# Half of the row tiles' sums of three modulation sets moved from VectorE to TensorE in a kernel's opening

## The chip, the cores and the metric

The kernel runs on one core of one Trainium2 chip. Its time is the device time of one execution in microseconds (us), and smaller is better. The core has a matrix engine (TensorE, PE in the profile; its weight loads are listed as PEld), a vector engine (VectorE, DVE), a scalar engine (ScalarE, ACT), GpSimd (POOL) and a queue engine (SyncE, SP) that issues most DMA transfers.

## The reference

The model is a trunk of two decoder layers on 512 tokens of width 2048, in float32. The first layer is differential attention, the second forgetting attention over shared keys and values. What the opening of the kernel computes is this:

```
c_act = silu(c)                                    # 2048 values
mod = c_act @ w_mod[0] + b_mod[0]                  # 2048 x 6144 weights
shift, scale, gate = split(mod, 3)
h = x * (1.0 + scale) + shift                      # 512 x 2048
proj = h @ a_w_in                                  # 2048 x 8192 weights; q, k, v, g
```

The product `c_act @ w_mod[0]` reads 2048 x 4096 weights for shift and scale alone, 33.5 MB, and uses each of them once. The projection behind it needs the finished `h`, one block of 128 columns at a time.

## The kernel before

Every large product is made of three float32r products of a high and a low part (`products`, lines 172 to 176), so a 128 x 128 block against 512 columns costs three matmuls. A weight tile comes by DMA as `wst`, ScalarE rounds it into `whi` (line 94) and VectorE subtracts to get `wlo` (line 95).

The opening (lines 438 to 644) has to make `h` before the projection can run, and runs both side by side. The 16 column blocks of shift and scale (`kt` = 0 to 15) are grouped into nine sets (`sets`, line 266): two of one block and seven of two blocks. For each set the opening does the following, in the steps that the code names:

- `load_mods` (line 462) loads the set's weights as tiles `sms` of 1 MB each. A tile of set 0 or 1 holds 8 of the 16 row tiles (128 rows each), so these sets have two `sms` tiles; a tile of the other sets holds 4, so they have four. Five `sms` buffers go round (`NBUF`), and a load waits in SP's queue until its buffer has been read. The block of `x` (`xt`) is loaded along with some of them.
- `mod_steps` (line 484) is a generator. Each step is one VectorE instruction that scales one row tile by its value of `c_act` and adds it to `sacc` (lines 496 and 498). `dv(n)` (line 506) takes up to n of these steps, and stops at the set after the one last summed.
- `mod_sums(i)` (line 512) takes what is left of the set's steps, and then adds `sacc` over its 128 partitions on TensorE, one matmul against a column of ones for each of shift and scale and each column block (line 528). `on_pe(i)` says how many of the 16 row tiles TensorE sums by itself: for these there is no VectorE step, but one matmul of a 128 x 128 weight block against a one-column `cact` (line 525). Before the change this is 8 row tiles for set 1 and none for the other sets.
- `mod_columns` (line 531) adds the bias on VectorE and gives `mcol` (line 534).
- `turn_x(kt)` transposes a block of `x` on TensorE (line 539), and ScalarE writes `hh` and `htmp` from it with scale and shift of `mcol` (lines 543 and 544). `lower_h` makes the low part `hl` on VectorE (line 548).
- `first_products(u, kt, ...)` (line 553) is 21 matmuls against 512 columns for head `u` (0 or 1) and block `kt`. Head 0 takes blocks 0 to 3, then head 1 blocks 0 to 7, and so on (`phases`).

The order of these steps is written out by hand in the string `START` (line 31): a digit is `dv`, `c` is sums, `m` is columns, `t` is turn, `l` is lower, `s` is the split of a weight tile, and `g` is the products of the next block. `turn` takes columns, and sums that are missing, by itself. VectorE's instructions keep exactly the order in which the string traces them; on the other engines a scheduler settles the order within the limits of the data. Each engine works its own instructions strictly in order. After the opening (from line 647 on) nothing depends on the string.

Of the kernel before, what the change touches and what calls it, by code (L numbers as in the profile page):

```python
# [10 lines left out]
F32 = mybir.dt.float32  # L11
# [5 lines left out]
P = 128  # L17
# [10 lines left out]
ET = mybir.EngineType  # L28


START = "cmtlssg6c6t1lgcst4g3tsl9sggts8sl6s2gtggts7lgsstlgg2s7gstl2ss9gsgtslgg5stgg6lsstg2gss8sggt2g4l4sgstctslggtslssggssgggg"
LAM_INIT = 0.8 - 0.6 * math.exp(-0.0)


# [76 lines left out]
def tile_yoco(  # L111
# [44 lines left out]
    def acc_bank(name="acc"):  # L156
        return ps.tile([P, 512], F32, name=name, tag="acc", bufs=4)
# [281 lines left out]
    with tc.tile_pool(name="start", bufs=2, reuse_waits="tile") as sp, tc.manual_schedule(engines={ET.DVE}):  # L439
# [3 lines left out]
        def load_x(q, f0, f1):  # L443
            if f0 == 0:
                xts[q] = sp.tile([P, TB, T], F32, name="xt", tag="xt", bufs=2)
            src = x[:, 512 * q + f0 : 512 * q + f1]
            nc.sync.dma_start(xts[q][:, :, f0:f1], src.rearrange("(b p) f -> p b f", p=P))

        def on_pe(i):
            return 8 if i == 1 else 0  # L450


        tiles = []
# [6 lines left out]
        NBUF = 5  # L460

        def load_mods(upto):
            while state["next"] < min(upto, len(tiles)):
                i, k, nr = tiles[state["next"]]
                k0, nk = sets[i]
                t = sp.tile([P, nr, 2, nk * P], F32, name="sms", tag="sms", bufs=NBUF)
                step = nr // 2 if i < 2 else nr
                for kq in range(0, nr, step):
                    for v in range(2):
                        rows = w_mod[0, (k + kq) * P : (k + kq + step) * P, v * D + k0 * P : v * D + (k0 + nk) * P]  # L470
                        nc.sync.dma_start(t[:, kq : kq + step, v, :], rows.rearrange("(k p) n -> p k n", p=P))
                loaded[i, k] = t
                state["next"] += 1
                if k == 0:
                    if k0 == 0:
                        load_x(0, 0, P)
                    elif k0 == 1:
                        load_x(0, P, T)
                    elif k0 % 4 == 0:
                        load_x(k0 // 4, 0, T)  # L480

        accs = {}

        def mod_steps():
            for n, (i, k, nr) in enumerate(tiles):
                k0, nk = sets[i]
                load_mods(n + NBUF)
                if k >= KT - on_pe(i):
                    continue
                if k == 0:  # L490
                    accs[i] = sp.tile([P, 2, 2 * P], F32, name="sacc", tag="sacc", bufs=2)
                acc = accs[i][:, :, : nk * P]
                for kq in range(nr):
                    w, sc = loaded[i, k][:, kq, :, :], cact[:, k + kq : k + kq + 1]
                    if k + kq == 0:
                        V.tensor_scalar(acc, w, sc, None, op0=ALU.mult)
                    else:
                        V.scalar_tensor_tensor(acc, w, sc, acc, op0=ALU.mult, op1=ALU.add)  # L498
                    yield i

        load_mods(2)
        ws.load(2)
        steps = mod_steps()
        ahead = [next(steps)]

# [6 lines left out]
        def mod_sums(i):  # L512
            k0, nk = sets[i]
            nr = 8 // nk
            dv(-1)
            state["set"] = i + 1
            load_mods(max(n for n, t in enumerate(tiles) if t[0] == i) + 1)
            pm = tr_bank()
            for v in range(2):
                for j in range(nk):  # L520
                    js = slice(j * P, (j + 1) * P)
                    dst = pm[:, nk * v + j : nk * v + j + 1]
                    for k in range(KT - on_pe(i), KT):
                        kr = k // nr * nr
                        PE.matmul(
                            dst, loaded[i, kr][:, k - kr, v, js], cact[:, k : k + 1], start=k == KT - on_pe(i), stop=False
                        )
                    PE.matmul(dst, accs[i][:, v, js], ones[:, 0:1], start=on_pe(i) == 0, stop=True)
            return pm
# [20 lines left out]
        acc = {}  # L550
# [71 lines left out]

        for tok in START:
            if tok.isdigit():
# [391 lines left out]
    npool, n, nstats = zp  # L1016
# [81 lines left out]
    acc = [acc_bank() for _ in range(TB)]  # L1098
# [277 lines left out]
```

## Time and profile before

| | |
|---|---|
| time, median of 3 runs | 1996.07 us (1995.78 to 1996.25) |
| the profiled execution's own time | 1992.9 us |
| its span | 1991.1 us |
| TensorE busy | 1955.8 us, 98% of the span |
| VectorE busy | 1320.8 us, 66% |
| ScalarE busy | 708.2 us, 36% |
| TensorE's granted clock, mean | 0.995 of full speed |

In the views below, the first two numbers of a timeline row are the start and the length in us; then come the engine, the line of the code, the operation, the tile written and those read, and the count. In square brackets stands how long the engine sat idle ahead of the row and what ended that. In a table by stage the columns are the stretch, its length, each engine's busy time with its count of instructions, the clock that TensorE was granted, the share of time in which the DMA engines were busy, and GB/s. Float32 matmuls against one column are recorded as two instructions each.

### The profile page before, as it was taken

The page shows a single profiled execution, that of the slowest core. Times are in us where ns is not written, and L with a number is a line of the kernel's source. Part 1 is how long each engine was busy: PE and PEld are TensorE (multiplying, and loading weights), DVE is VectorE, ACT ScalarE, POOL GpSimd, SP SyncE. Part 2 cuts the span into 40 slices and gives each one's busy share as a digit, 9 for nine tenths or more (in the row PEclk, how much of TensorE's full clock was granted, in tenths as well). Part 3 has the DMA queues.
Part 4 walks back from the last instruction along what each step waited for, and adds up shares of the span by engine and source line. Part 5 has one row for each costly group of instructions (what it writes and reads, how often), then busy time and mean ns, then how long its engine had stood idle before and what let it go on. Part 6 is the DMA issues. An engine that isn't in the chain of part 4 may idle for free.

```text
span 1991.1 us, 24748 instructions
## 1 busy us (share of the span) xinstructions
PE 1955.8 (98%) x9079; PEld 1618.8 (81%) x9079; DVE 1320.8 (66%) x2404; ACT 708.2 (36%) x1217; POOL 2.2 (0%) x10
## 2 busy tenths in 40 slices
PE   5999999999999999999999999999999999999997
PEld 4888888888888888888888888888888888888886
DVE  7885667777777778853575656565555555576657
ACT  2432445333332334431273222224343434353123
POOL 0000000000000000000000000000000000000000
PEclk8999999999999999999999999999999999999999
DMA  9993444666667576552336676663333232232622
GB/s 344 348 317 96 143 149 157 191 213 201 211 191 227 186 232 203 189 170 98 127 128 227 233 239 199 223 212 127 96 96 100 96 105 92 96 120 96 232 92 106
DMA packets 259029, 343.81 MB, mean 173 GB/s; under 512 B 18614, under 2 KB 163404, under 8 KB 258140
## 3 DMA queue, kind: packets, MB, share of 16 engines
q1 hardware_dynamic: 256528, 338.02, 52.0%
q10 hardware_dynamic: 2380, 4.21, 0.6%
q8 instruction: 71, 1.16, 0.2%
q14 instruction: 50, 0.41, 0.1%
HBM read 329.51 MB, written 12.66 MB: 172 GB/s over the span
## 4 chain that ended last, share of the span: by engine, by line
PE 91%; DVE 4%; DMA 2%; issue 1%; ACT 1%; SPq 0%; DVEq 0%; ACTq 0%
PE acc L174 26%; PE acc L176 26%; PE acc L175 26%; PE sc L174 2%; PE sc L175 2%; PE sc L176 2%; PE o L176 1%; PE o L174 1%; PE o L175 1%; PE tr L1228 1%; DMA ms<-in_w_mod_dram 1%; DVE wlo L95 1%; DMA ms<-in_kv_w_mod_dram 1%; DVE sacc L498 1%; DVE macc L391 1%
## 5 line engine op out<-in xcount | busy, mean ns | idle before, releaser
L95 DVE TENSOR_TENSOR wlo<-wst,whi 128x1024 fp32r<-128x1024 f32 (+2 forms) x322 | 384.2, 1195 | 335.5 <-ACT whi L94 319.5
L94 ACT CAST whi<-wst 128x1024 fp32r<-128x1024 f32 (+2 forms) x322 | 331.8, 1031 | 662.2 <-PE acc L176 347.9
L174 PE MATMUL acc<-whi,hh 128*128 128x512 f32 x1232 | 484.3, 396 | 1.8 <-DVE sg L695 1.0
L175 PE MATMUL acc<-wlo,hh 128*128 128x512 f32 x1232 | 480.9, 390 | 0.1
L176 PE MATMUL acc<-whi,hl 128*128 128x512 f32 x1232 | 480.5, 390 | 0.0
L174 PE MATMUL acc<-hh,whi 128*128 128x512 f32 x1184 | 471.1, 398 | 0.6 <-DVE sg L695 0.6
L175 PE MATMUL acc<-hl,whi 128*128 128x512 f32 x1184 | 462.3, 390 | 0.0
L176 PE MATMUL acc<-hh,wlo 128*128 128x512 f32 x1184 | 461.7, 390 | 0.0
L174 PEld LDWEIGHTS acc<-whi,hh 128*128 128x128 f32 x1232 | 232.5, 189 | 48.5 <-DVE ztmp L926 1.2
L176 PEld LDWEIGHTS acc<-whi,hl 128*128 128x128 f32 x1232 | 231.3, 188 | 49.2
L175 PEld LDWEIGHTS acc<-wlo,hh 128*128 128x128 f32 x1232 | 231.6, 188 | 45.4 <-DVE wlo L95 0.5
L176 PEld LDWEIGHTS acc<-hh,wlo 128*128 128x128 f32 x1184 | 222.3, 188 | 48.8
L174 PEld LDWEIGHTS acc<-hh,whi 128*128 128x128 f32 x1184 | 222.6, 188 | 43.8 <-issue 1.9
L175 PEld LDWEIGHTS acc<-hl,whi 128*128 128x128 f32 x1184 | 222.8, 188 | 38.9
L391 DVE SCALAR_TENSOR_TENSOR macc<-ms,cact,macc 128x512 f32<-128x512 f32 x300 | 224.1, 747 | 37.6 <-DMA ms<-in_kv_w_mod_dram 21.8
L498 DVE SCALAR_TENSOR_TENSOR sacc<-sms,cact,sacc 128x512 f32<-128x512 f32 (+1 forms) x127 | 89.5, 704 | 5.0 <-DMA sms<-in_w_mod_dram 1.4
L725 ACT ACTIVATE e<-e,mn 128x128 f32<-128x128 f32 (+3 forms) x64 | 36.1, 564 | 120.6 <-DVE mn L721 120.5
L1217 ACT ACTIVATE eb<-eb,mnb 128x128 f32<-128x128 f32 (+1 forms) x64 | 36.0, 563 | 95.3 <-DVE mnb L1214 94.2
L1214 DVE CUSTOM_DVE_ANT_0 eb<-sc,biasb 128x128 f32<-128x128 f32 (+1 forms) x64 | 31.4, 490 | 55.3 <-PE sc L176 55.3
L1232 DVE TENSOR_TENSOR pTl<-tr,pTh 128x128 fp32r<-128x128 f32 (+1 forms) x64 | 31.1, 487 | 25.3 <-ACT pTh L1231 24.8
L391 DVE SCALAR_TENSOR_TENSOR macc<-msk,cact,macc 128x512 f32<-128x512 f32 x60 | 45.0, 749 | 1.4
L1231 ACT CAST pTh<-tr 128x128 fp32r<-128x128 f32 (+1 forms) x64 | 27.2, 424 | 44.3 <-PE tr L1228 43.5
(260 smaller groups left out, 1773.3 us busy)
## 6 DMA issues: line engine op xcount, KB each, us to landing
wst<-in_a_w_in_dram SPq DMA_DIRECT2D x240, 256.0 KB, 3.8
ms<-in_w_mod_dram SPq DMA_DIRECT2D x64, 512.0 KB, 4.4
ms<-in_kv_w_mod_dram SPq DMA_DIRECT2D x64, 512.0 KB, 4.2
wst<-in_kv_w_dram SPq DMA_DIRECT2D x64, 512.0 KB, 3.9
wst<-in_b_w_in_dram SPq DMA_DIRECT2D x128, 256.0 KB, 2.9
sms<-in_w_mod_dram SPq DMA_DIRECT2D x56, 512.0 KB, 6.9
wst<-in_a_w_out_dram SPq DMA_DIRECT2D x32, 512.0 KB, 3.7
msk<-in_w_mod_dram SPq DMA_DIRECT2D x64, 256.0 KB, 5.5
```

What stands on the lines that cost most here:

```text
L94: self.nc.scalar.copy(hi[:, :, :w], st[:, :, :w])
L95: self.nc.vector.tensor_tensor(lo[:, :, :w], st[:, :, :w], hi[:, :, :w].bitcast(F32), op=ALU.subtract)
L174: PE.matmul(dst, lhs[0], rhs[0], start=start, stop=False)
L175: PE.matmul(dst, lhs[0], rhs[1], start=False, stop=False)
L176: PE.matmul(dst, lhs[1], rhs[0], start=False, stop=stop)
L391: ins = V.scalar_tensor_tensor(acc, w, cact[:, kt : kt + 1], acc, op0=ALU.mult, op1=ALU.add)
L498: V.scalar_tensor_tensor(acc, w, sc, acc, op0=ALU.mult, op1=ALU.add)
L725: S.activation(e[:, :w], e[:, :w], AF.Exp, bias=mn, scale=-1.0, accum_out=rs)
L1214: V.tensor_tensor_reduce(out=e[:, :w], in0=sc[:, :w], in1=bias[:, :w], scale=-1.0, scalar=3.0e38, op0=ALU.add, op1=ALU.min, accum_out=mn)
L1217: S.activation(e[:, :w], e[:, :w], AF.Exp, bias=mn, scale=-1.0, accum_out=rs)
L1231: S.copy(pTh[:, 0 : i + 1, ts], src)
L1232: V.tensor_tensor(pTl[:, 0 : i + 1, ts], src, pTh[:, 0 : i + 1, ts].bitcast(F32), op=ALU.subtract)
```

## The change

`on_pe` returns 8 for the sets 0, 1 and 2 instead of for set 1 alone. For set 0 (one block) and set 2 (two blocks) half of the row tiles, the rows 1024 to 2047, are therefore summed by TensorE at line 525 (527 after the change), and VectorE has 8 steps fewer in each. The generator `mod_steps` now yields ahead of each operation and not behind it, so loads, the allocation of `sacc` and the operation itself are all traced when the step is taken. The head of `START` is written anew; from the characters `sl9sggts8sl6s` on it is as it was.

```diff
-START = "cmtlssg6c6t1lgcst4g3tsl9sggts8sl6s2gtggts7lgsstlgg2s7gstl2ss9gsgtslgg5stgg6lsstg2gss8sggt2g4l4sgstctslggtslssggssgggg"
+START = "cmtlssgc6t2lgcsst3lg3tsl9sggts8sl6s2gtggts7lgsstlgg2s7gstl2ss9gsgtslgg5stgg6lsstg2gss8sggt2g4l4sgstctslggtslssggssgggg"
...
         def on_pe(i):
-            return 8 if i == 1 else 0
+            return 8 if i < 3 else 0
...
         def mod_steps():
             for n, (i, k, nr) in enumerate(tiles):
                 k0, nk = sets[i]
-                load_mods(n + NBUF)
                 if k >= KT - on_pe(i):
                     continue
-                if k == 0:
-                    accs[i] = sp.tile([P, 2, 2 * P], F32, name="sacc", tag="sacc", bufs=2)
-                acc = accs[i][:, :, : nk * P]
                 for kq in range(nr):
+
+                    yield i
+                    if kq == 0:
+                        load_mods(n + NBUF)
+                    if k + kq == 0:
+                        accs[i] = sp.tile([P, 2, 2 * P], F32, name="sacc", tag="sacc", bufs=2)
+                    acc = accs[i][:, :, : nk * P]
                     w, sc = loaded[i, k][:, kq, :, :], cact[:, k + kq : k + kq + 1]
                     if k + kq == 0:
                         V.tensor_scalar(acc, w, sc, None, op0=ALU.mult)
                     else:
                         V.scalar_tensor_tensor(acc, w, sc, acc, op0=ALU.mult, op1=ALU.add)
-                    yield i
```

In the built program this gives TensorE 48 more one-column matmuls (16 in set 0 and 32 in set 2), and VectorE 16 fewer steps. The instruction orders differ as follows. In SP's queue six loads of `wst` stand ahead of the `sms` tiles of row tiles 4 to 11 of set 2; before they stood behind them. On VectorE the bias of set 1 stands behind the second step on the tile of row tiles 4 to 7 of set 2, and all eight VectorE steps of set 2 then end four instructions ahead of that set's bias; the first step of set 3 stands behind the bias of set 2, ahead of which it stood before. On TensorE the transposes for block 3 stand behind the products of block 2, where they stood in the midst of them; and the sums of set 3 stand 78 large matmuls behind those of set 2, where it was 59.

## The prediction

> **What bounds the kernel now.** I read the page's head first, then TensorE's waits in two halves, then the opening's timeline engine by engine, then the granted clock by stage.
>
> ```profile
> span 1991.1 us, 24748 instructions
> PE 1955.8 (98%) x9079; PEld 1618.8 (81%) x9079; DVE 1320.8 (66%) x2404; ACT 708.2 (36%) x1217; POOL 2.2 (0%) x10
> ```
>
> TensorE is the bound: it is busy all but 35 us of the span. A change can only pay if it takes work from TensorE or shortens its few waits. Its waits in the first 43.4 us, and then from there to 220 us, beyond the opening's last set:
>
> ```profile
> PE tr L528 <- DVE sacc L498: 11.1, 1, 11.1
> PE sc L174 <- ACT hh L543: 3.3, 3, 1.6
> ...
> PE tr L539 <- DVE mcol L534: 1.9, 3, 1.0
> PE tr L528 <- ACT whi L94: 1.0, 1, 1.0
> ...
> PE sc L174 <- ACT hh L543: 0.9, 1, 0.9
> ```
>
> The last row is all there is after 43.4 us (it is the wait that ends at 43.34). So from the products of block 2, which start at 43.34, TensorE never stops, and whatever delays that start delays the end by as much, unless later work shrinks. The question is only when these products start after the change, and whether TensorE stays fed behind them.
>
> TensorE's own rows of the stretch:
>
> ```profile
> 14.40 0.99 PE L528 MATMUL tr<-ones,sacc 128*128 128x1 f32 x4 [11.07 <-DVE sacc L498]
> ...
> 14.60 0.78 PE L528 MATMUL tr<-ones,sacc 128*128 128x1 f32 x3
> ...
> 14.82 0.57 PE L528 MATMUL tr<-ones,sacc 128*128 128x1 f32 x2
> ...
> 16.04 1.12 PE L539 MATMUL tr<-ident,xt 128*128 128x128 f32 x4 [0.65 <-DVE mcol L534]
> 18.02 1.22 PE L174 MATMUL sc<-hh,whi 128*128 128x512 f32 x2 [0.87 <-ACT hh L543]
> ...
> 21.17 0.63 PE L175 MATMUL o<-hl,whi 128*128 128x512 f32 x1
> 21.60 1.05 PE L176 MATMUL sc<-hh,wlo 128*128 128x512 f32 x2
> ...
> 23.28 0.39 PE L175 MATMUL acc<-wlo,hh 128*128 128x512 f32 x1
> 23.51 0.39 PE L176 MATMUL acc<-whi,hl 128*128 128x512 f32 x1
> ...
> 25.10 1.84 PE L525 MATMUL tr<-cact,sms 128*128 128x1 f32 x16
> 26.80 0.36 PE L528 MATMUL tr<-ones,sacc 128*128 128x1 f32 x2
> 27.02 1.93 PE L525 MATMUL tr<-cact,sms 128*128 128x1 f32 x16
> 28.81 0.36 PE L528 MATMUL tr<-ones,sacc 128*128 128x1 f32 x2
> 30.18 1.11 PE L539 MATMUL tr<-ident,xt 128*128 128x128 f32 x4 [1.01 <-DVE mcol L534]
> 32.87 1.22 PE L174 MATMUL sc<-hh,whi 128*128 128x512 f32 x2 [1.58 <-ACT hh L543]
> ...
> 39.19 0.39 PE L176 MATMUL acc<-whi,hl 128*128 128x512 f32 x1
> 40.53 1.02 PE L528 MATMUL tr<-ones,sacc 128*128 128x1 f32 x8 [0.96 <-ACT whi L94]
> 41.81 0.66 PE L539 MATMUL tr<-ident,xt 128*128 128x128 f32 x4 [0.26 <-DVE mcol L534]
> 43.34 1.22 PE L174 MATMUL sc<-hh,whi 128*128 128x512 f32 x2 [0.87 <-ACT hh L543]
> ```
>
> The reader sees a chain that repeats: sums, bias, transposes, ScalarE, products. Sixteen one-column instructions and two more against the ones take 1.92 us in set 1 (25.10 to 27.02), 0.107 us each. Those of set 0 start at 14.40, 14.60 and 14.82, some 0.21 us apart: half as fast. The large matmuls do likewise, 0.43 us apart at 21.17 and 0.23 at 23.28. The clock by stage (its column reads 1.00 ahead of 22.7, but these distances say half):
>
> ```profile
> 22.72:26.14 3.42, 3.42 (x22) 1.00 1.09 385
> 26.14:29.55 3.41, 3.03 (x28) 1.00 1.09 386
> 29.55:32.96 3.41, 1.20 (x5) 0.50 1.10 375
> 32.96:36.38 3.42, 3.42 (x8) 0.50 1.09 384
> 36.38:39.79 3.41, 3.19 (x14) 1.00 1.08 397
> 39.79:43.20 3.41, 1.68 (x12) 1.00 1.07 387
> 43.20:46.61 3.41, 3.27 (x8) 0.50 1.09 380
> ```
>
> In these rows the clock changes at the ends of stretches of 3.41 us, and follows the stretch just past. After 32.96 to 36.38, full of large matmuls, it is full. After 26.14 to 29.55 it is halved, though TensorE was busy for 3.03 of 3.41 us, nearly all of it with one-column matmuls. So these rows say that one-column sums don't hold the clock. The DMA engines are saturated all along (1.07 to 1.10, about 385 GB/s).
>
> **Set 0.** VectorE loses 8 steps of 128x256, 4.13 us by this row, in which the second tile had landed by about 10.1 us in its first half:
>
> ```profile
> 10.12 4.13 DVE L498 SCALAR_TENSOR_TENSOR sacc<-sms,cact,sacc 128x256 f32<-128x256 f32 x8 [0.19 <-DMA sms<-in_w_mod_dram]
> ```
>
> TensorE gains 16 matmuls, 32 instructions, which with the four it had run at the halved clock: 36 x 0.213 = 7.7 us. Starting between 9.3 (one DMA earlier) and 10.1, they end at 17.0 to 17.8, against 15.39 before. About 0.35 us comes back, because before the bias stood behind a VectorE step. Block 0's products start about 1.3 us later (19.3); as the clock rises at 22.7 either way, half of that is left when the sums of set 1 start: 25.8 for 25.10. These sums end at about 29.8 (before 29.17).
>
> **Set 1's bias.** Here the delay so far doesn't count, since something later takes over. The bias stands behind two steps on row tiles 4 to 7 of set 2, and their load now stands behind six loads of `wst`. When it lands can be read from a transfer of before:
>
> ```profile
> 31.31 0.83 ACT L94 CAST whi<-wst 128x768 fp32r<-128x768 f32 x1 [12.67 <-DMA wst<-in_a_w_in_dram]
> ...
> 29.97 0.15 DVE L534 TENSOR_TENSOR mcol<-tr,bcol 128x2 f32<-128x2 f32 x1
> ...
> 34.13 6.25 DVE L498 SCALAR_TENSOR_TENSOR sacc<-sms,cact,sacc 128x512 f32<-128x512 f32 x8
> ```
>
> By 31.3 the queue had moved two `sms` tiles (2.10 MB) and one `wst` tile (0.39 MB) behind row tiles 0 to 3 of set 2. After the change the wanted tile is complete after three `wst` tiles (1.31 MB) and itself (1.05 MB), 0.13 MB less: 0.35 us earlier, 30.95. Two steps at 0.78 us (6.25 / 8) give 32.5, and the bias falls at about 32.45 instead of 29.97. Transposes follow 0.21 us later (29.97 to 30.18) and take 1.11, and 0.86 us lies between their end and the products (17.16 to 18.02). Products start at 34.65 instead of 32.87: only 1.8 of the 2.5 us, since before a cast of ScalarE (the row at 31.31) stood in between, which is early now. If the clock rises at 36.4 as before, 4 matmuls run at 0.43 and 17 at 0.2275: end at 40.3. If it rises one stretch later, at 39.8, the end is 41.9.
>
> **Set 2, the main term.** VectorE loses 8 steps, the 6.25 us above, and has its half done by 34.1. All the weights are there by 36.4: two more tiles, 2.10 MB at 385 GB/s, behind the one of 30.95. But TensorE reaches these sums only at 40.3, when before the last VectorE step had just ended too (40.3). It now has 36 matmuls, 72 instructions, in place of 8: nothing covers them, because the next block's transposes wait for the bias behind them. At the full clock they take 72 x 0.109 = 7.9 us, at the half 72 x 0.213 = 15.3. From the row of 26.14 to 29.55 I take a fall at the end of the stretch that starts at 39.8: 27 instructions to 43.2 and 45 x 0.213 = 9.6 us behind it. End at 52.9, against 41.55. Bias, transposes at half clock and ScalarE take 2.2 us (15.39 to 18.02 less the 0.35), so block 2's products start at 55.1 in place of 43.34: **+11.8 us**. Both run their first 3.4 us or so at the half clock; no difference.
>
> **Block 3's transposes** stand behind these products, no longer among them, so the wait for ScalarE is open (0.87 us in the row at 43.34): **+0.9 us**.
>
> **Behind that.** The work that VectorE does between two biases, beside the steps:
>
> ```profile
> 40.70 0.95 DVE L95 TENSOR_TENSOR wlo<-wst,whi 128x768 fp32r<-128x768 f32 x1
> ...
> 45.38 0.68 DVE L548 TENSOR_TENSOR hl<-htmp,hh 128x512 fp32r<-128x512 f32 x1
> 45.99 1.22 DVE L95 TENSOR_TENSOR wlo<-wst,whi 128x1024 fp32r<-128x1024 f32 x1
> ```
>
> Its order puts all of set 3 behind set 2's bias, so its 16 steps start at 53 and not at 40.3, and SP's queue is held: the loads that reuse the buffers of row tiles 8 to 15 of set 2 wait for TensorE's sums to end, all later ones behind them. TensorE has 78 large matmuls between these sums and the next, 17.7 us, so set 3 is covered (16 steps, 12.3 us, and 3.3 for two low parts and two splits). For set 4 the order leaves 61, 13.9 us with 1.7 of transposes and sums, against some 16.2 us of VectorE's work (one split more): short by about half a microsecond, and the low part of one weight tile stands behind eight steps of that set (6.2 us and two splits of 1 us against some 7.3 us of TensorE's work: a wait of 1). Later sets are near balance. The lower end is 0, as the trace of before shows no such wait; the upper end is some 5, five sets with a microsecond each. I take the two shortfalls, 1.5, and 1 more for the DMA queue that stood still: **+2.5 us**.
>
> **The sum.** 11.8 + 0.9 + 2.5 = 15.2 us. The set 0 delay is inside the first term. The arrangement behind the opening is the same, and TensorE is saturated there, so nothing gives it back. The profiled execution took 1992.9 us, of which 1.8 lie around its span; the median of the runs is 3.2 us higher. The difference is added to the median: 1996.07 + 15 = 2011.
>
> **The rivals.** *The sums hold the clock.* The Trainium skill's page "TensorE: Matmul & The Clock Gate", section "What's actually happening", ties the full clock to how busy the engine has been in the last window, without a difference by width. As a mechanism of this kernel: 72 instructions at 0.109 from 40.3 end at 48.15; warm, 1.8 us follow as before (41.55 to 43.34), so products start at 49.9, 6.6 us late, and they save about 1.6 us, as their first 3.4 us don't run at half rate. With 0.9 and 2.5 behind it: +8.4, 2004.5. The fall at 29.55 after a stretch 89% busy speaks against it.
>
> *One-column matmuls are cheaper than the row.* At half its price, 0.054 us, set 2's sums end at 44.2 and the products start at 46.0, warm: 2.7 less 1.6, and 3.4 behind it: +4.5, 2000.6. The 16 in 1.70 us at the full clock (25.10 to 26.80) speak against it: they are the same shape from the same kind of tile. The same page, section "Back-to-back issue gap", gives a floor of about 25 ns for narrow matmuls; by it, as an estimate, the 72 would take 1.8 us and the sum would come to about +2.4.
>
> *Faster.* VectorE was late, and TensorE sums while it would wait. The place is the stretch from 29.2 to 43.3, in which TensorE stood idle for 4.7 us (the five brackets from 30.18 to 43.34). It pays if set 2's sums end before 41.55, so that at 0.109 they begin before 33.7: 6.6 us ahead of what I find, and before the last tile lands. Were it so, the 1.1 us between 39.4 and 40.5 and a microsecond more would be saved: 1994. Decisive is that TensorE reaches these sums at 40.3 with nothing left to wait for.
>
> *No change:* the added sums fit wholly into waits, and VectorE's 10.4 us fewer (4.13 + 6.25) pay for the rest: 1996. It needs an idle TensorE of 10 us between 29 and 43; there are 4.7.
>
> *Worse:* the order behind 53 us falls out of step with the held DMA queue, each set waiting for its loads by 1 to 2 us: +20, 2016 to 2020.
>
> **How the numbers follow.** The likeliest case has 0.62 and spans 2007 to 2016 (15.2 with the later waits 0 or 5, the clock's phase 3 us either way). The warm sums have 0.22 (2002 to 2007), the cheap ones 0.04, faster 0.04, no change 0.03, worse 0.05. The range from 2003 to 2016.5 leaves out faster, none, cheap, worse and a little of the warm case, under 0.2. Repeated runs differ by 0.02%, and about 0.2% (4 us) is what a measurement tells from no change. All cases but faster, none and half of the cheap are slower by more: slower 0.92, same 0.05, faster 0.03.
>
> **What would show it.** Right: some 7 us of one-column matmuls from about 9.5 us; set 1's bias at 32 to 33 behind a wait for `sms`; 72 one-column instructions from about 40 that take 10 to 13 us, with a granted clock of 0.5 from 43 on; block 2's products at 53 to 56; VectorE idle behind the bias of set 2; DMA below 1.0 between 50 and 60; a few waits of TensorE for `sacc` or `wlo` between 70 and 180. Wrong: set 2's sums over by 42, or a full clock through them, or an end less than 5 us later although block 2 starts 10 us late, which would mean that something behind the opening has slack that I don't see.

## The result and the profile after

The changed kernel takes 2010.67 us (median of 6 runs, 2008.68 to 2014.10); the kernel before took 1996.11 in the same series (1995.78 to 1997.05). The ratio is 1.0074, with a 95% interval from 1.0061 to 1.0087: the change makes the kernel slower by 14.6 us. The profiled execution took 2011.02 us.

The head of the page, and then TensorE's waits from 0 to 70 us and from 70 to 230 us:

```profile
span 2009.2 us, 24919 instructions
PE 1974.9 (98%) x9175; PEld 1636.9 (81%) x9175; DVE 1312.4 (65%) x2388; ACT 708.3 (35%) x1217; POOL 2.2 (0%) x10
```
```profile
PE tr L527 <- DVE sacc L501: 6.3, 1, 6.3
PE tr L541 <- DVE mcol L536: 3.7, 3, 3.2
PE sc L174 <- ACT hh L545: 3.5, 4, 0.9
...
PE acc L175 <- DVE wlo L95: 0.8, 1, 0.8
```

TensorE has 96 instructions more and is busy for 19.1 us more, for a span that is 18.1 us longer. On balance, then, the time did not go into waiting. It went into TensorE's own rows in the opening:

```profile
9.69 3.54 PE L527 MATMUL tr<-cact,sms 128*128 128x1 f32 x16 [6.33 <-DVE sacc L501]
13.10 0.56 PE L530 MATMUL tr<-ones,sacc 128*128 128x1 f32 x2
13.52 3.55 PE L527 MATMUL tr<-cact,sms 128*128 128x1 f32 x16
16.93 0.56 PE L530 MATMUL tr<-ones,sacc 128*128 128x1 f32 x2
...
33.90 1.12 PE L541 MATMUL tr<-ident,xt 128*128 128x128 f32 x4 [3.19 <-DVE mcol L536]
35.88 1.22 PE L174 MATMUL sc<-hh,whi 128*128 128x512 f32 x2 [0.87 <-ACT hh L545]
...
43.20 1.84 PE L527 MATMUL tr<-cact,sms 128*128 128x1 f32 x16
44.90 0.36 PE L530 MATMUL tr<-ones,sacc 128*128 128x1 f32 x2
45.12 1.93 PE L527 MATMUL tr<-cact,sms 128*128 128x1 f32 x16
46.91 0.36 PE L530 MATMUL tr<-ones,sacc 128*128 128x1 f32 x2
47.13 2.86 PE L527 MATMUL tr<-cact,sms 128*128 128x1 f32 x16
49.85 0.56 PE L530 MATMUL tr<-ones,sacc 128*128 128x1 f32 x2
50.27 3.55 PE L527 MATMUL tr<-cact,sms 128*128 128x1 f32 x16
53.69 0.56 PE L530 MATMUL tr<-ones,sacc 128*128 128x1 f32 x2
54.51 1.11 PE L541 MATMUL tr<-ident,xt 128*128 128x128 f32 x4 [0.25 <-DVE mcol L536]
56.49 1.22 PE L174 MATMUL sc<-hh,whi 128*128 128x512 f32 x2 [0.87 <-ACT hh L545]
...
65.22 0.73 PE L174 MATMUL sc<-hh,whi 128*128 128x512 f32 x2 [0.87 <-ACT hh L545]
```

The sums of set 2 last from 43.20 to 54.25, 11.05 us, where they took 1.02. No row among them waits for anything. Block 2's products start at 56.49 for 43.34 (13.15 us late), block 3's at 65.22 for 50.18 (15.04 late). The row of before for block 3:

```profile
50.18 0.62 PE L174 MATMUL sc<-hh,whi 128*128 128x512 f32 x2
```

The clock in the stretches of set 2's sums:

```profile
41.07:44.49 3.42, 3.42 (x23) 1.00 1.08 389
44.49:47.90 3.41, 3.41 (x32) 1.00 1.10 380
47.90:51.31 3.41, 3.41 (x18) 0.50 0.53 187
51.31:54.73 3.42, 3.17 (x15) 0.50 0.39 115
```

In the second row TensorE is busy for all of 3.41 us with one-column matmuls, and at its end the clock is halved. In the two rows behind it the DMA engines work at half their share or less, since SP's queue is held until these sums have read their buffers (its longest wait for them is 7.1 us).

### The profile page after: what moved, and what is told of

Same layout as the page of the kernel before. It is cut to its first block, busy times and chain, and to the rows that moved or that the text cites. A ratio compares the mean times of both kernels' runs of the same rounds, so it can differ in the third digit from the quotient of the medians.

```text
span 2009.2 us, 24919 instructions
## 1 busy us (share of the span) xinstructions
PE 1974.9 (98%) x9175; PEld 1636.9 (81%) x9175; DVE 1312.4 (65%) x2388; ACT 708.3 (35%) x1217; POOL 2.2 (0%) x10
## 4 chain that ended last, share of the span: by engine, by line
PE 91%; DVE 4%; DMA 2%; SPq 1%; issue 1%; ACT 1%; DVEq 0%; ACTq 0%
PE acc L174 26%; PE acc L175 26%; PE acc L176 26%; PE sc L174 2%; PE sc L175 2%; PE sc L176 2%; PE o L174 1%; PE o L175 1%; PE o L176 1%; PE tr L1230 1%; DVE wlo L95 1%; DMA ms<-in_kv_w_mod_dram 1%; SPq L471 1%; DMA sms<-in_w_mod_dram 1%; DVE macc L391 1%
## 5 line engine op out<-in xcount | busy, mean ns | idle before, releaser
L391 DVE SCALAR_TENSOR_TENSOR macc<-ms,cact,macc 128x512 f32<-128x512 f32 x300 | 224.4, 748 | 34.2 <-DMA ms<-in_kv_w_mod_dram 18.1
L501 DVE SCALAR_TENSOR_TENSOR sacc<-sms,cact,sacc 128x512 f32<-128x512 f32 (+1 forms) x111 | 79.7, 718 | 6.5 <-DMA sms<-in_w_mod_dram 3.2
```

The source lines that it names most:

```text
L391: ins = V.scalar_tensor_tensor(acc, w, cact[:, kt : kt + 1], acc, op0=ALU.mult, op1=ALU.add)
```

## The experiments

**Which part costs.** Four kernels take the parts one by one. The first has set 2 back on VectorE:

```diff
-            return 8 if i < 3 else 0
+            return 8 if i < 2 else 0
```

> The changed kernel with set 2 back on VectorE (its 32 one-column matmuls gone, 8 VectorE steps back); set 0 and the new order stay. Before is 1996.1 us, the changed kernel 2010.7. Theory A, set 2's sums stand open on TensorE (11.8 of 15.2 us): block 2's products start near 45 us instead of 56.5, and the end is 1999 to 2002. Theory B, the new order itself costs most, whoever sums: the products of block 2 are early again, but the end stays above 2005, with new waits behind 60 us.

The second has only the new string and the new yield:

```diff
-            return 8 if i < 3 else 0
+            return 8 if i == 1 else 0
```

> The changed kernel with sets 0 and 2 both back on VectorE: only the new string and the new place of the yield are left. Theory A: the 3.4 us of the terms for block 3's transposes and for what stands behind, so 1998 to 2001, and block 2's products start at 43 to 45 us. Theory B (the order costs most): 2004 to 2008, with TensorE waiting for sacc or wlo between 60 and 180 us.

The third is the changed kernel with the `START` of the kernel before, and nothing else changed.

> The changed kernel with the old string: TensorE takes half of the sums of sets 0, 1 and 2, the order of steps is the old one. Theory A: 11.8 us of open sums remain, less the terms of the order, so 2007 to 2010, and block 2's products start at 53 to 57 us. Theory B: 1996 to 1999.

The fourth adds set 2's price to the kernel before, as work whose result nothing reads:

```diff
                     PE.matmul(dst, accs[i][:, v, js], ones[:, 0:1], start=on_pe(i) == 0, stop=True)
+                    if i == 2:
+                        spare = pm[:, 64 + nk * v + j : 65 + nk * v + j]
+                        for k in range(8, KT):
+                            PE.matmul(spare, loaded[i, k // nr * nr][:, k % nr, v, js], cact[:, k : k + 1], start=k == 8, stop=k == KT - 1)
```

> The kernel before with the price of set 2 alone: 32 one-column matmuls on the same weights are added to its sums in set 2 and write to a spare column that nothing reads; VectorE, the string and the loads stay as before. Theory A: 64 instructions at 0.107 us as far as the clock lasts and 0.213 behind it, 7 to 13.6 us, all of it open: 2004 to 2009, and the clock falls to half during or right after them. If one-column sums held the clock: +6.8 less up to 1.6, so about 2002, with a clock of 1.00 through them. If they were hidden: 1996 to 1997.

| kernel | median us (runs) | ratio to before, 95% interval |
|---|---|---|
| before, in this series | 1995.16 (18) | |
| set 2 on VectorE | 1999.05 (9) | 1.0022 [1.0012, 1.0032] |
| order alone | 1998.10 (10) | 1.0016 [1.0006, 1.0025] |
| split with the old string | 2008.98 (4) | 1.0070 [1.0055, 1.0085] |
| dead sums in the kernel before | 2007.39 (4) | 1.0061 [1.0046, 1.0076] |

All four times lie where theory A has them (the third inside its 2007 to 2010). Block 2's products start at 46.64 us in the first kernel and at 45.64 in the second, later than theory A had them (near 45, and 43 to 45). The new order alone costs some 3 us; set 2's one-column matmuls, added to a kernel that is otherwise untouched, cost 12. Theory B falls. The clock by stage of the kernel with the dead sums:

```profile
38.18:41.59 3.41, 3.18 (x19) 1.00 1.06 400
41.59:45.01 3.42, 3.42 (x33) 1.00 1.09 385
45.01:48.42 3.41, 3.41 (x18) 0.50 0.53 186
48.42:51.83 3.41, 3.41 (x17) 0.50 0.00 0
```

Again a stretch that is full of one-column matmuls (the second row, with the first sums at 40.81) is followed by half the clock; and the loads stop altogether in the fourth. The order's cost is open rows too. In the profile of the kernel with the order alone, TensorE waits for VectorE's steps of set 2, and block 3's transposes stand behind block 2's products:

```profile
41.67 1.02 PE L530 MATMUL tr<-ones,sacc 128*128 128x1 f32 x8 [2.30 <-DVE sacc L501]
...
45.64 1.22 PE L174 MATMUL sc<-hh,whi 128*128 128x512 f32 x2 [0.87 <-ACT hh L545]
...
52.39 0.60 PE L541 MATMUL tr<-ident,xt 128*128 128x128 f32 x4
53.86 0.73 PE L174 MATMUL sc<-hh,whi 128*128 128x512 f32 x2 [0.87 <-ACT hh L545]
```

Block 2's products thus start 2.3 us later than before, and block 3's 3.7 us. From there to 230 us TensorE waits for nothing. Theory A's 3.4 us for the order was near the measured 2.9, but most of it, the 2.5 us behind the opening's sums, did not arise where theory A had it; that the number fits is luck.

**Is it the width that loses the clock?** The dead sums are replaced by wide matmuls of about the same length at full clock:

```diff
+                    if i == 2:
+                        for k in range(10):
+                            PE.matmul(pm[:, 128:512], Hh[0][:, 0:P], Hh[0][:, 0:384], start=True, stop=True)
```

> The kernel before with 40 dead matmuls of 128x384 in set 2's sums, 6.9 us at full clock, in place of the 32 dead one-column ones, which took 6.8 us by the same clock and brought 2007.4 against 1995.2. Theory A, one-column matmuls don't hold the clock and wide ones do: no fall to 0.5 in or behind these sums, block 2's products start near 50 us and save the 1.6 us of their first stretch: 1999.5 to 2001.5. If the clock fell for another reason (the waits around the sums): 2005 to 2008 again.

It took 2000.68 us (5 runs) against 1994.37, ratio 1.0031 [1.0019, 1.0044]. The stretches around the sums, which run from 42.5 to 50.6:

```profile
42.20:45.60 3.40, 3.31 (x21) 1.00 1.09 383
45.60:49.00 3.40, 3.40 (x23) 1.00 1.09 380
49.00:52.40 3.40, 2.27 (x15) 1.00 1.09 385
```

The clock stays up through them and the products behind. Block 2's products start at 52.39, where near 50 was expected: the sums began 2.0 us later than before (42.53 for 40.53), as set 1's bias had come at 31.80 instead of 29.97, behind waits for `sms`. The lengths at full clock can be read from the first rows of the dead one-column sums and of the wide ones:

```profile
41.02 1.93 PE L532 MATMUL tr<-cact,sms 128*128 128x1 f32 x16
42.81 0.36 PE L528 MATMUL tr<-ones,sacc 128*128 128x1 f32 x2
```
```profile
42.74 1.98 PE L531 MATMUL tr<-hh 128*128 128x384 f32 x10
44.56 0.28 PE L528 MATMUL tr<-ones,sacc 128*128 128x1 f32 x2
```

Sixteen one-column instructions take 1.79 us and ten wide ones 1.82, so 7.2 and 7.3 us in all; yet the first cost 12.2 us and the second 6.3. The wide ones differ in more than the width: they are float32r, one instruction each, and read the same weights every time, where the sums are float32 and read new weights. That the single column alone loses the clock is therefore not shown. This also bears on the Trainium skill's page "TensorE: Matmul & The Clock Gate", section "What's actually happening", where a busy engine is at full clock: if busy means the time in which matmuls run, the rows of this case differ from it (3.41 of 3.41 us busy, and 0.50 behind it).

**Half the size.** Set 2 with a quarter of its row tiles on TensorE:

```diff
-            return 8 if i < 3 else 0
+            return (8, 8, 4)[i] if i < 3 else 0
```

> The changed kernel with a quarter of set 2's row tiles on TensorE in place of half: 16 one-column matmuls instead of 32, 4 VectorE steps back. Without set 2's split the end was 1999.05 us, with half of it 2010.67. If the price went by the count alone, half of the 11.6 us: 2004.9. By theory A it is less than half, since 40 instructions at 0.107 us (4.3 us) fit into the time that the clock still lasts, and a wait for the second half's load is not in the way: block 2's products start near 49 us, and the end is 2001.5 to 2004.

2003.42 us (4 runs), 1.0043 [1.0026, 1.0060]. That is 4.4 us above the kernel without set 2's split, and another 7.2 us come with the second half. The sums take 5.3 us (41.63 to 46.97), and the clock falls only at 45.12, when some 30 of their 40 instructions are through; block 2's products start at 49.21 and run at half clock until 55.36.

**What set 0 costs.** I expected next to nothing from it.

```diff
-            return 8 if i < 3 else 0
+            return 8 if i in (1, 2) else 0
```

> The changed kernel with set 0 back on VectorE; set 2 stays split and the new order stays. Theory A: the delay of set 0 is swallowed by the later bias of set 1, and set 2's sums stay open, so 2008 to 2011, within 2 us of the changed kernel. If set 0's 7.7 us of sums at half clock were on the path: 2004 to 2007.

2005.83 us (4 runs), 1.0057 [1.0042, 1.0072]: 4.8 us less than the changed kernel, so this expectation of theory A was a miss. SP's rows show that more than the sums had changed. Here are the changed kernel, and then the one with set 0 on VectorE:

```profile
14.55 6.34 SPq L471 DMA_DIRECT2D sms<-in_w_mod_dram  x6
20.93 3.33 SPq L47 DMA_DIRECT2D wst<-in_a_w_in_dram  x6
```
```profile
14.42 7.33 SPq L471 DMA_DIRECT2D sms<-in_w_mod_dram  x8
21.79 4.47 SPq L47 DMA_DIRECT2D wst<-in_a_w_in_dram  x6
```

Two loads, the tile with row tiles 4 to 7 of set 2, are ahead of the six `wst` loads again. Loads are now traced with VectorE's first step on a tile. The second tile of set 0 has no step on VectorE any more, and so its call, which loads up to the sixth tile, is gone; a later tile's step makes up for it, too late. To part the two effects, the next kernel keeps set 0 on TensorE and gives the call back (and those of the tiles of sets 1 and 2 that have no VectorE step):

```diff
                 if k >= KT - on_pe(i):
+                    load_mods(n + NBUF)
                     continue
```

> The changed kernel with one line more: for a tile that has no VectorE steps, the loads of the tile five further on are traced where the generator passes it, as in the kernel before, so that the load of set 2's row tiles 4 to 7 stands ahead of the six loads of wst again. The arithmetic stays as in the changed kernel. Taking set 0 off TensorE had saved 4.9 us (2005.83 against 2010.67) and had moved this load too. Theory D, the load is what costs: set 1's bias comes at 30 to 31 us in place of 33.7, and the end is 2004.5 to 2007. If the 7.7 us of sums of set 0 at half clock cost by themselves: the end stays at 2009 to 2011.

2005.50 us (4 runs), 1.0054 [1.0040, 1.0068], with set 1's bias at 30.92. Its rows on VectorE, after those of the changed kernel:

```profile
32.23 1.54 DVE L501 SCALAR_TENSOR_TENSOR sacc<-sms,cact,sacc 128x512 f32<-128x512 f32 x2 [2.48 <-DMA sms<-in_w_mod_dram]
33.69 0.15 DVE L536 TENSOR_TENSOR mcol<-tr,bcol 128x2 f32<-128x2 f32 x1
```
```profile
27.10 3.90 DVE L502 SCALAR_TENSOR_TENSOR sacc<-sms,cact,sacc 128x512 f32<-128x512 f32 x5
30.92 0.16 DVE L537 TENSOR_TENSOR mcol<-tr,bcol 128x2 f32<-128x2 f32 x1
```

And its rows on TensorE:

```profile
53.79 1.22 PE L174 MATMUL sc<-hh,whi 128*128 128x512 f32 x2 [0.87 <-ACT hh L546]
...
58.03 0.60 PE L542 MATMUL tr<-ident,xt 128*128 128x128 f32 x4
...
60.77 0.61 PE L174 MATMUL sc<-hh,whi 128*128 128x512 f32 x2
```

So the late load costs, as theory D has it, and set 0's 7.7 us of sums on TensorE cost nothing that these runs resolve (2005.50 with them, 2005.83 without). How much the load costs is less sure. The time is 5.2 us below the changed kernel's; but above the kernel before, each in its own series, the two stand 14.56 and 11.13 us, a difference of 3.4, and their intervals overlap. In the profiles block 2's products start 2.7 us earlier (53.79 for 56.49), and block 3's 4.5 (60.77 for 65.22). The added line changed TensorE's order too: block 3's transposes stand among block 2's products again (58.03), so the wait of 0.87 us is gone, and the half clock lasts 3.5 us into these products instead of 5.1.

With set 2 on VectorE, set 0 cost only 0.95 us (1999.05 against 1998.10), though its load was late there too. Block 1's products start 2.6 us later (35.46 for 32.85), but block 2's only 1.0 (46.64 for 45.64), since in both kernels TensorE waits for VectorE's steps of set 2, until 43.13 and 41.67. The costs don't add up one by one; what a delay costs depends on which engine is late behind it.

**Why the runs spread.** The changed kernel's runs lie 5.4 us apart.

> The changed kernel once more, for a second profile: its runs spread over 5.4 us, those of the kernel before over 1.3 in the same series. Theory C, the clock's 3.41 us stretches lie differently in each execution, and so do the one-column sums in them: this profile shows its falls and rises shifted by up to 3.4 us against the first, with the same sums at another mean duration, and the span moves with the time spent at half clock. If the spread came from the loads: the same clock, and longer waits for sms.

The two runs took 2009.81 and 2012.40 us, the second with the profile (span 2010.6, 1.4 us longer than in the first profile). Its opening shows the signs of both theories: the clock fell at 47.10 in place of 47.90, and set 2's sums took 11.73 us in place of 11.05; set 1's bias came at 34.26 in place of 33.69, behind a wait for `sms` of 3.26 in place of 2.48. But none of this is left when block 3's products start, at 65.17 in place of 65.22. The 1.4 us come much later. A wait of 1.93 us for `sg` left TensorE busy for only 1.49 us of the stretch from 835.57 to 838.99, and the stretch behind it, to 842.40, ran at half clock; its large matmuls stood 0.43 us apart, which is some 1.6 us more than at full clock. The first profile has no such stretch. So here it was the clock, but not at the sums, and two executions don't settle the 5.4 us of six.

**A cheaper step on VectorE.** In the kernel before, VectorE waits 2.7 us for block 1's `htmp` while set 2's weights lie there.

```diff
-START = "cmtlssg6c6t1lgcst4g3t...
+START = "cmtlssg6c6t5lgcst4g3t...
```

> The kernel before with one digit of the string changed (1 to 5), so that VectorE runs four steps of set 2, whose weights are there, ahead of block 1's low part, for which it waits 2.7 us. Set 2's sums end 0.8 us earlier at most, as its last tile lands at 36.4 and four steps stand behind it: 0.5 to 2 us faster, the more if the next products thereby miss a stretch at half clock, so 1993 to 1995 where before reads 1995.2. If the low part is missed on TensorE instead: 0 to 1 us slower.

1994.93 us (11 runs) against 1994.37, ratio 1.0000 [0.9991, 1.0009]: no difference, and not the gain that I expected. It went as in the other branch, the low part missed on TensorE. VectorE then waited for the last tile instead, until 36.84, and TensorE for a later low part:

```profile
36.84 3.11 DVE L498 SCALAR_TENSOR_TENSOR sacc<-sms,cact,sacc 128x512 f32<-128x512 f32 x4 [1.95 <-DMA sms<-in_w_mod_dram]
```
```profile
40.58 0.95 PE L528 MATMUL tr<-ones,sacc 128*128 128x1 f32 x8
43.31 0.73 PE L174 MATMUL sc<-hh,whi 128*128 128x512 f32 x2 [0.87 <-ACT hh L543]
47.04 0.50 PE L175 MATMUL sc<-hl,whi 128*128 128x512 f32 x1 [1.40 <-DVE hl L548]
```

## Why the prediction was right

The forecast was 2011 and the time 2010.67; sign, size and main cause were right: set 2's one-column sums stand open on TensorE and lose the clock. By its steps:

- **Set 0:** foreseen were 7.7 us of sums from 9.3 to 10.1 and an end at 17.0 to 17.8. They ran from 9.69 to 17.49, and set 1's sums began at 26.64 where I had 25.8. That the delay of these sums would be swallowed was right, as the kernel with the load put back shows.
- **Set 1's bias:** foreseen at 32.45, measured 33.69. The mechanism, the six `wst` loads ahead, was right. The step that was too small is the landing: I let the tile be complete at 30.95, and VectorE waited until 32.23. I had counted the bytes ahead as if loads landed one after another at 385 GB/s; why this one came later was not tried. I also listed the load as a part of the new order, when it hangs on set 0's split: its own share, 2.7 us at the start of block 2's products, is larger than the 1.8 us I gave the delay of block 1's.
- **Set 2, the main term:** foreseen from 40.3 to 52.9, measured 43.20 to 54.25. The start was later, for the bias and because the clock rose at 41.07 instead of 36.4. The length came out shorter (11.05 for 12.6), as the clock fell at 47.90 and not at 43.2: the stretches lay otherwise in this execution, and the stretch up to 44.49 held large matmuls until 43.20. Block 2's products were 13.15 us late, where I had 11.8.
- **Block 3's transposes:** a wait of 0.87, as foreseen. The rest of the step from 13.15 to 15.04 is half clock that lasted until 61.55, 5.1 us into block 2's products and not 3.4.
- **Behind that:** foreseen 2.5 us, seen a single wait of 0.8 between 70 and 230 us. It is a wait for `wlo`, which the forecast had at 1 us; the half microsecond for `sacc` and the microsecond for the DMA queue did not arise. This term was too large, and made good for the main one, which was too small. The held DMA queue is there (0.53 and 0.39 of the time busy), but no wait of TensorE, VectorE or ScalarE between 54 and 150 us ended with a load.
- **The signs:** they came 0.5 to 5 us later than named: set 1's bias at 33.69 (32 to 33), half clock from 47.90 (43), block 2's products at 56.49 (53 to 56). VectorE stood idle for 11.8 us, ahead of set 2's bias and not behind it.
- **The sum:** up to 230 us the profiles show 13.15 + 1.89 + 0.8 = 15.8 us, where I had 15.2. The profiled span grew by 18.1 us and the median by 14.6, since the profiled execution of before, 1992.9 us, lay 3.2 below its median. Behind 230 us TensorE waits 5.2 us in the changed kernel (3.1 of them for `sg`) and 3.2 in the kernel before; in the kernel with one digit changed, which is as fast as before, it waits 3.0 for `sg` as well. With terms that were off by 1 to 2 us either way, and runs that lie 5.4 us apart, it is luck that forecast and time differ by only 0.3 us.
- **The chances:** those of the cases add up to 0.91 for slower and 0.04 for faster, where I wrote 0.92 and 0.03.

Of the rivals, the sums that hold the clock fall by the clock behind them, 0.50; the wide matmuls, which do hold it, cost 6.3 us, where that rival has 5.0 for the sums (6.6 less 1.6). Cheaper one-column matmuls fall by the rows: 16 instructions in 1.70 us at full clock, as before. The gain and "no change" fall by the result, and "worse" by the single wait between 70 and 230 us.

## What to carry to other kernels

Where one engine sets the end, work moved to it is free only in its waits; find the time at which that engine reaches the moved work, and if nothing is left to wait for there, the whole length counts. A float32 matmul against a single column took two instructions of 0.107 us here, almost as long as a float32r one against 512 columns (0.2275 us), and these sums didn't keep the clock up, so a few microseconds of them also slowed what followed. When a step disappears from one engine, see what else was traced with it: here a load went with it, and set 1's bias came 2.8 us later for it.

## What was not expected of the hardware

A stretch of 3.41 us in which TensorE was busy for 3.41 us, all with one-column matmuls, ended at half the clock in the changed kernel and in the one with dead sums. 40 matmuls of 128x384 in the same place kept it full. The prediction took the fall from a stretch that was 89% busy; these two had no gap at all, so gaps alone do not explain it. Nor did set 0's sums raise the clock from half, though they ran without a gap from 9.69 to 17.49 in the changed kernel: block 0's matmuls behind them stand 0.43 us apart until about 24. And four fifths of a stretch were not enough even with large matmuls: in the kernel with a quarter of set 2, TensorE was busy with them for 2.74 us of the stretch from 48.53 to 51.95 and the clock stayed at half; it rose only at 55.36, behind a stretch that was full of them.

The changed kernel's six runs lie 5.4 us apart and the six of before in the same series 1.3; but 18 runs of before in a later series lie 4.7 us apart (1992.0 to 1996.7), so that the change makes the spread larger is not shown. In the changed kernel's six runs the mean granted clock goes from 0.993 in the two shortest to 0.991 in the longest. By an estimate from these rounded figures, 0.002 of 2010 us is 4 us, most of the 5.4; but in the kernel with the order alone the clock does not sort the runs (0.995 at 1996.46, 0.996 at 1998.90). What makes the spread is open.
